# A streaming encoder step: 24 column units of the input projection as 12 pairs with seven quarter products, in a stage of their own ahead of the attention

## The chip, the cores and the metric

The kernel runs on one core of one Trainium2 chip. The core has a matrix engine (TensorE, PE in the profile, with its weight loads as PEld), a vector engine (VectorE, DVE), a scalar engine (ScalarE, ACT), a general one (GpSimd, POOL) and SyncE (SP), whose queue here issues most of the DMA transfers. Each engine works through its own instructions in order, and semaphores order the engines among each other. The metric is the device time of one execution in microseconds. Lower is better.

## What is computed

One layer of an encoder for 1024 prompt tokens and 64 sample tokens, all in float32. The tokens are normalised and multiplied by one input projection of 1024 x 6144. Its columns are the queries, keys, values and gate of two attention branches, then two channel gates.

```
def project(x, norm_w, w_in, q_norm_w, k_norm_w):
    h = rms_norm(x, norm_w) @ w_in
    sb_q, sb_k, sb_v, sb_z, cb_q, cb_k, cb_v, cb_z, g_sb, g_cb = jnp.split(h, SPLIT_POINTS, axis=-1)
    ...

def stick_breaking(q, k, v, q_pos, k_pos):
    z = jnp.einsum("bqhd,bkhd->bhqk", q, k).astype(jnp.float32) * ATTN_SCALE
    causal = k_pos[None, :] < q_pos[:, None]
    log_beta = jax.nn.log_sigmoid(z)
    log_keep = jnp.where(causal, jax.nn.log_sigmoid(-z), 0.0)
    suffix = lax.cumsum(log_keep, axis=3, reverse=True) - log_keep
    w = jnp.where(causal, jnp.exp(log_beta + suffix), 0.0)
    return jnp.einsum("bhqk,bkhd->bqhd", w.astype(v.dtype), v)

def merge(x, o_sb, z_sb, o_cb, z_cb, g_sb, g_cb, w_proj_sb, w_proj_cb, w_out):
    b_sb = (o_sb.reshape(lead + (WIDTH_SB,)) * jax.nn.silu(z_sb)) @ w_proj_sb
    b_cb = (o_cb.reshape(lead + (WIDTH_CB,)) * jax.nn.silu(z_cb)) @ w_proj_cb
    h = jax.nn.sigmoid(g_sb) * b_sb + jax.nn.sigmoid(g_cb) * b_cb
    return x + h @ w_out
```

The second branch ("cb") is a softmax over a band of at most 640 keys with a learned bias by distance. The keys and values of both branches are outputs too, in their natural layout (token by token).

## The kernel before

Every product keeps float32 accuracy by splitting each factor in a high and a low part, and by multiplying three times: high x high, high x low, low x high. The high part is an ACT copy, the low part a subtraction on DVE or POOL.

**Phase 1** (line 153 on) loads the tokens in nine tiles, normalises and transposes them into `xhl`, which stays on chip with the model dimension on the partitions (high and low, two halves of four blocks each, 1088 token columns). Beside that it computes eight groups of 256 columns (`NB`, line 160) in natural layout: the values of both branches, and the queries and keys of the second, which are normed per head, transposed and stored to DRAM (`d_qT`, `d_kT`).

**Units.** The other 32 blocks of 128 columns are "units" (`make_units`, line 120): k, q and the two gates z of each head pair, and the channel gates. A unit computes the transposed result: for each of three token ranges `CH` it runs 8 blocks x 3 matmuls, 24 of 384 or 320 columns, so 72 in all (line 563). Units are not a stage. They are a generator, `run_fill` (line 556), that gives one matmul at a time as a filler; after the last unit it continues with the first branch's output projection (`proj_units`, line 622, matmuls in line 661; 288 of them for each branch). A unit's weights are loaded two units ahead and split one unit ahead.

**Attention** (line 870 on) goes through 144 units of work: first branch ("sb", stick-breaking), then second ("cb", chunk band), each with four head pairs p, nine query tiles t (the sample tile first) and two heads. For unit i it emits in this order: `qk(i)` (scores, line 725 and 726; in sb the two sigmoids, lines 728 and 729; in cb the bias with a running minimum, line 731, and the exponential, line 735), half of the fillers, the product with the values of a finished tile pair (`av`, line 817), the transposes of unit i-2 (`tr`, line 777, copied to `wT` in turn by ACT and DVE, lines 786 and 788), `mid(i)` (in sb a scan and a multiply on DVE, lines 745 and 746; in cb a reciprocal and a scaling, lines 748 and 749), and the other fillers. The number of fillers follows the number of keys. In sb a filler's result goes straight to the place where it is used (`ev_k`, `ev_q`); `ev_k` also transposes k back for the natural-layout output, through the one buffer `ko` (line 519). In cb the tiles are loaded from DRAM by `load_q` and `load_k`. `until` makes sure that a head pair's own units are done before its attention begins.

**Phases 4 and 5** (line 910 on): the second branch's attention output is loaded, split (`make_og`, line 614, whose subtractions are line 620) and projected, with the rest of the fillers between; then the output projection with the residual (lines 990 to 992).

## Time and profile before

| what | value |
|---|---|
| runs of the kernel | 1035.84, 1037.40, 1037.94 us; median 1037.4 |
| profiled execution | span 1034.6 us from first to last instruction |
| granted TensorE clock | 0.999 of full speed on average |
| phase 1, from the start to the first filler | 230.2 us |
| weight splits on POOL, line 98 (tile `wlo`) | 51 operations, 127.6 us |
| matmuls of the units, line 563 | 2304 |

The profile is one execution. Its page lists each engine's busy time, the chain of work that ended last, and groups of equal instructions: line, engine, operation, out<-in, count | busy us, mean ns of one | idle time of the engine just ahead of them and who ended it. Busy times of matmuls overlap, as they are pipelined: the time that one costs is the distance from start to start, not its listed duration. A wait is put down to the one that came last. Idle time of an engine that does not set the end costs nothing.

### The profile page before, as it was taken

How to read it: one execution, taken by the hardware profiler on the slowest of the kernel's cores; microseconds unless marked ns; L12 is line 12 of the kernel's file. 1: busy time of each engine (PE TensorE's matmuls, PEld its weight loads, DVE VectorE, ACT ScalarE, POOL GpSimd, SP SyncE). 2: the span in 40 equal slices, each digit the busy share in tenths (PEclk: the TensorE clock that was granted, in tenths of full speed). 3: DMA queues.
4: the chain of work that ended last, by engine and by line, in shares of the span. 5: the costliest groups of instructions: out<-in, count | busy, mean ns of one | idle time of the engine just before them, and what ended most of it. 6: DMA issues, size and time to landing. Idle time of an engine off the chain costs nothing.

```text
span 1034.6 us, 19354 instructions
## 1 busy us (share of the span) xinstructions
PE 1014.8 (98%) x7412; PEld 968.4 (94%) x7412; DVE 543.9 (53%) x1069; ACT 418.7 (40%) x942; POOL 255.2 (25%) x277
## 2 busy tenths in 40 slices
PE   6999999999999999999999999999999999999998
PEld 5999999999999989999999999998988898999998
DVE  5416656402476556657655645565557685674111
ACT  5534443212454435444444454444445433552000
POOL 3227666202221111212121111101103211453110
PEclk9999999999999999999999999999999999999999
DMA  7654453745547323723384354665576834554322
GB/s 237 213 187 151 163 191 128 267 136 165 160 112 192 96 69 102 206 60 95 92 211 122 107 144 131 165 169 161 162 204 185 224 92 139 187 163 149 101 93 71
DMA packets 159660, 155.23 MB, mean 150 GB/s; under 512 B 23184, under 2 KB 144912, under 8 KB 159440
## 3 DMA queue, kind: packets, MB, share of 16 engines
q1 hardware_dynamic: 142800, 136.17, 44.2%
q10 hardware_dynamic: 16768, 17.83, 5.7%
q8 instruction: 58, 0.95, 0.4%
q14 instruction: 34, 0.28, 0.1%
HBM read 90.77 MB, written 49.81 MB: 136 GB/s over the span
## 4 chain that ended last, share of the span: by engine, by line
PE 91%; SPq 3%; DMA 2%; DVE 1%; ACT 1%; issue 1%; POOL 0%; ACTq 0%; DVEq 0%
PE acc L563 33%; PE acc L357 18%; PE acc L661 9%; PE o L817 7%; PE pt L777 6%; PE z L726 3%; PE z L725 3%; PE acc L992 3%; PE acc L991 3%; PE acc L990 3%; SPq L49 2%; DMA wrawx<-in_w_in_dram 1%; PE pk L301 1%; PE pt L229 1%; DMA d_ccbT<-hc 1%
## 5 line engine op out<-in xcount | busy, mean ns | idle before, releaser
L563 PE MATMUL acc<-xh,whi 128*128 128x384 f32 (+1 forms) x768 | 255.5, 333 | 0.1
L563 PE MATMUL acc<-xh,wlo 128*128 128x384 f32 (+1 forms) x768 | 255.3, 332 | 0.0
L563 PE MATMUL acc<-xl,whi 128*128 128x384 f32 (+1 forms) x768 | 254.8, 332 | 0.0
L98 POOL TENSOR_TENSOR wlo<-wraw,whi 128x1024 fp32r<-128x1024 f32 x51 | 127.6, 2501 | 440.2 <-ACT whi L91 386.1
L563 PEld LDWEIGHTS acc<-xh,wlo 128*128 128x128 f32 x768 | 144.8, 189 | 1.3
L563 PEld LDWEIGHTS acc<-xl,whi 128*128 128x128 f32 x768 | 144.5, 188 | 1.3
L563 PEld LDWEIGHTS acc<-xh,whi 128*128 128x128 f32 x768 | 144.5, 188 | 1.2 <-ACT sg L550 0.3
L745 DVE TENSOR_TENSOR_SCAN kp<-kp,imp 64x576 f32<-64x576 f32 (+8 forms) x72 | 110.6, 1536 | 5.1 <-ACT kp L728 5.1
L735 ACT ACTIVATE be<-be,sm 128x640 f32<-128x640 f32 (+5 forms) x72 | 50.8, 706 | 106.6 <-DVE sm L731 106.4
L728 ACT ACTIVATE kp<-z 128x384 f32<-128x384 f32 (+6 forms) x112 | 53.8, 480 | 97.3 <-PE z L726 87.6
L777 PE MATMUL pt<-ident,be 128*128 128x128 f32 (+2 forms) x608 | 88.8, 270 | 0.9 <-DVE wT L788 0.6
L786 ACT ACTIVATE wT<-pt 128x512 f32<-128x512 f32 (+3 forms) x104 | 52.9, 509 | 82.5 <-PE pt L777 81.6
L788 DVE COPY wT<-pt 128x256 f32<-128x256 f32 (+3 forms) x104 | 46.0, 442 | 70.3 <-PE pt L777 69.9
L777 PEld LDWEIGHTS pt<-ident,be 128*128 128x128 f32 (+2 forms) x608 | 68.7, 139 | 11.6 <-issue 7.1
L357 PE MATMUL acc<-whi,xh 128*128 128x256 f32 x256 | 75.2, 296 | 0.0
L357 PE MATMUL acc<-wlo,xh 128*128 128x256 f32 x256 | 71.7, 282 | 0.0
L357 PE MATMUL acc<-whi,xl 128*128 128x256 f32 x256 | 71.5, 281 | 0.0
L357 PE MATMUL acc<-whix,xh 128*128 128x256 f32 x256 | 70.9, 279 | 0.0
L357 PE MATMUL acc<-whix,xl 128*128 128x256 f32 x256 | 70.6, 278 | 0.0
L91 ACT ACTIVATE whi<-wraw 128x1024 fp32r<-128x1024 f32 x52 | 55.0, 1059 | 38.4 <-DVE y L996 35.8
L357 PE MATMUL acc<-wlox,xh 128*128 128x256 f32 x256 | 70.5, 277 | 0.0
L746 DVE TENSOR_TENSOR be<-be,kp 64x576 f32<-64x576 f32 (+8 forms) x72 | 62.3, 865 | 8.8
(157 smaller groups left out, 2168.7 us busy)
## 6 DMA issues: line engine op xcount, KB each, us to landing
wraw<-in_w_in_dram SPq DMA_DIRECT2D x40, 512.0 KB, 4.9
sq<-hl SPq DMA_DIRECT2D x32, 192.0 KB, 4.5
sq<-d_qT SPq DMA_DIRECT2D x32, 192.0 KB, 3.6
xt<-in_x_prompt_dram SPq DMA_DIRECT2D x8, 512.0 KB, 5.6
wrawx<-in_w_in_dram SPq DMA_DIRECT2D x8, 512.0 KB, 4.3
d_kT<-hl SPq DMA_DIRECT2D x8, 512.0 KB, 4.7
d_qT<-hl SPq DMA_DIRECT2D x8, 512.0 KB, 4.8
ks<-d_kT SPq DMA_DIRECT2D x16, 256.0 KB, 4.6
```

Of the source, the lines that this page charges most:

```text
L91: A.activation(h, raw, AF.Copy)
L98: (eng or G).tensor_tensor(out=l, in0=raw, in1=h[:].bitcast(F32), op=OP.subtract)
L357: TE.matmul(ps, x, w, start=m == 0, stop=m == len(steps) - 1)
L563: TE.matmul(ps[:, :b - a], w[:, k], xk(x, k)[:, a:b], start=k == 0 and n == 0, stop=k == KT - 1 and n == 2)
L661: TE.matmul(ps[:, :n], w[:, p, cw], g[:, a:e], start=p == 0 and m == 0, stop=p == NPAIR - 1 and m == 2)
L728: A.activation(kp[:r, x:y], z[:r, :m], AF.Sigmoid, scale=-0.125)
L735: A.activation(be[:r, :n], be[:r, :n], AF.Exp, bias=kp[:r, j:j + 1], scale=-1.0, accum_out=kp[:r, 2:3])
L745: V.tensor_tensor_scan(kp[:r, n - 1::-1], kp[:r, n - 1::-1], im[:, ::-1], 0.0, op0=OP.mult, op1=OP.add)
L746: V.tensor_tensor(out=be[:r, :n], in0=be[:r, :n], in1=kp[:r, 1:n + 1], op=OP.mult)
L777: TE.transpose(pt[:kr, x, :r], be[:r, kb * 128:kb * 128 + kr], ident[:r, :r])
L786: A.activation(w[:, sl:sl + m, q0:q0 + r], pt[:, :m, :r], AF.Copy)
L817: TE.matmul(o[hd * 64:hd * 64 + 64, c0:c1], vv[:kr, kb, hd * 64:hd * 64 + 64], wT[b, p, j, hd, s // 4][:kr, s % 4, c0:c1], start=si == 0, ...
```

## The change

The 12 k, q, z and first-gate pairs (two neighbouring units each, 256 columns) leave the fillers. Each pair is a product of a 256 x 1024 weight block and 1024 x 1088 tokens. It is cut in two along each side (columns 128 + 128, model dimension 512 + 512, tokens 544 + 544), and the four quarter results come from seven products of quarters instead of eight, after a scheme that adds and subtracts the factors first and the results afterwards. For this:

- the token columns of `xhl` are reordered (`xc`), so that each half holds 512 prompt and 32 sample tokens; `pieces` finds the token ranges again when results are stored;
- `make_t` forms four combinations of the token quarters on DVE, with their splits, beside the last groups of phase 1; phase 1's column groups and the step that prepares the bias rows change places for it, and the pool of phase 1 is closed early;
- `prep` forms the weight combinations on POOL and splits them (ACT, POOL), five products ahead; `load_raw` loads the raw halves;
- a new stage between phase 1 and the attention runs 12 x 7 products of 24 matmuls (12 with 256, 12 with 288 columns), in six PSUM banks; ACT and DVE combine the results, and `emit` stores them to DRAM, for k also in natural layout through `ko`. `up` is a pool of three buffers where no other number is given; `psF` has two buffers;
- the first branch's attention loads q and k from DRAM like the second, and `ev_k`, `ev_q`, `ev_silu`, `until` are gone. Eight units (the second channel gate) remain as fillers: one ahead of the attention, six in the first branch, one in the second with all 288 matmuls of the first output projection. The last unit is held back until the second branch has begun (`late["sb"]`). In the first branch ACT makes all copies to `wT`.

```diff
-        NB = [1024, 1280, 2560, 2816, 2048, 2304, 3072, 3328]
+        NB = [1024, 2560, 2816, 2048, 2304, 1280, 3072, 3328]
...
+        def make_t(tm, pool):
...
+            def sub(a, b, k):
+                d = pool.tile([128, HF], F32, name="d")
+                V.tensor_tensor(out=d, in0=x(0, *a[:1], k, a[1]), in1=x(0, *b[:1], k, b[1]), op=OP.subtract)
+                V.tensor_tensor(out=d, in0=d, in1=x(1, *a[:1], k, a[1]), op=OP.add)
+                V.tensor_tensor(out=d, in0=d, in1=x(1, *b[:1], k, b[1]), op=OP.subtract)
+                return d
...
+        def prep(n):
+
+            i, s = divmod(n, 7)
...
+            def total(x, y, op):
+                d = ws.tile([128, 4, 128], F32, name="ws")
+                G.tensor_tensor(out=d, in0=x, in1=y, op=op)
+                return d[:]
+
+            if s == 0:
+                src = r1[:, :, a]
+            elif s == 1:
+                sums[1] = total(r1[:, :, b], r2[:, :, b], OP.add)
+                sums[2] = src = total(sums[1], r1[:, :, a], OP.subtract)
...
+            A.activation(t[:, 0], src, AF.Copy)
+            G.tensor_tensor(out=t[:, 1], in0=src, in1=t[:, 0].bitcast(F32), op=OP.subtract)
+            blk[n] = t
+            if s == 4:
+                load_raw(2 * i + 3)
+            elif s == 6:
+                load_raw(2 * i + 4)
...
-                if (i, ti) == (4, 4):
+                if (i, ti) == (3, 8):
                     load_rb()
-                if i == 6 and ti > 0:
+                if i == 4 and ti > 0:
                     make_rb(ti - 1)
...
+        LEAD = 5
+        later = []
+
+        def soon(n, f):
+            later.append([n, f])
+
+        def step():
+            for e in later[:]:
+                e[0] -= 1
+                if e[0] < 0:
+                    later.remove(e)
+                    e[1]()
...
+        def emit(i, w, half, c, src, ps):
+
+            kind, _, arg = pairs[i]
+            n = XC[c][1] - XC[c][0]
...
+            h = up.tile([128, 2, 288], F32R, name="hl", bufs=2)
+            A.activation(h[:, 0, :n], src[:, :n], AF.Copy)
+            V.tensor_tensor(out=h[:, 1, :n], in0=src[:, :n], in1=h[:, 0, :n].bitcast(F32), op=OP.subtract)
+            p = arg + w
+            dst = (d_kT if kind == "k" else d_qT)["sb"][p]
+            soon(0, lambda: stores(rdma, half, c, h[:, :, :n], dst[:]))
+            if kind == "q":
+                return
...
+            def out():
+                pt = psF.tile([128, 512], F32, name="acc")
+                ko = up.tile([128, 3, 128], F32, name="ko", bufs=1)
+                cols = slice(p * 128, (p + 1) * 128)
+                for t in range(2):
+                    TE.transpose(pt[:, t * 128:(t + 1) * 128], kf[:, t * 128:(t + 1) * 128], ident)
+                if c == 1:
+                    TE.transpose(pt[:32, 256:384], kf[:, 256:288], ident)
+                    A.activation(ko[:32, 2], pt[:32, 256:384], AF.Copy)
+                    SP.dma_start(o_sbk_s[32 * half:32 * half + 32, cols], ko[:32, 2])
+                A.activation(ko[:, :2], pt[:, :256].rearrange("p (t c) -> p t c", c=128), AF.Copy)
+                a = half * 512 + c * 256
+                SP.dma_start(o_sbk_p[a:a + 256, cols].rearrange("(t q) c -> q t c", q=128), ko[:, :2])
+            soon(1, out)
...
+        BANK = "1231223"
+        for i in range(len(pairs)):
+            bank, s1, u2, u3 = {}, {}, {}, {}
+            for s in range(7):
+                n = 7 * i + s
+                prep(n + LEAD)
...
+                step()
+                w = blk.pop(n)
+                for c, (a, b) in enumerate(XC):
+                    m = b - a
+                    if s < 3:
+                        bank[BANK[s], c] = psB.tile([128, 512], F32, name=f"b{BANK[s]}{c}")
+                    ps = bank[BANK[s], c]
+                    for k in range(4):
+                        for e, (hl_, x) in enumerate(((0, 0), (0, 1), (1, 0))):
+                            TE.matmul(ps[:, :m], w[:, hl_, k], right[s](x)[:, k, a:b], start=s < 3 and k == 0 and e == 0,
+                                      stop=k == 3 and e == 2, skip_group_check=s > 2)
+                    if s == 0:
+                        s1[c] = up.tile([128, 288], F32, name="s1")
+                        A.activation(s1[c][:, :m], ps[:, :m], AF.Copy)
+                    elif s in (1, 4):
+                        u = up.tile([128, 288], F32, name="u2" if s == 1 else "u3")
+                        (u2 if s == 1 else u3)[c] = u
+                        V.tensor_tensor(out=u[:, :m], in0=ps[:, :m], in1=s1[c][:, :m], op=OP.add)
+                    elif s == 3:
+                        emit(i, 0, 0, c, ps, True)
...
     def fill(n):
+        n += owed[0]
+        owed[0] = 0
         while n > 0:
+            if prog[0] == len(units) - 2 and "sb" not in late:
+                owed[0] = n
+                return
...
-                if flip[0] % 2:
+                if flip[0] % 2 or b == "sb":
                     A.activation(w[:, sl:sl + m, q0:q0 + r], pt[:, :m, :r], AF.Copy)
...
-    until(1)
-    fill(48)
-    FP = 170
-    n_sb = 72 * FILL_SB - 48
-    n_cb = 72 * (len(units) - 2 - FILL_SB) + FP
+    fill(72)
+    FP = 288
+    n_sb = 72 * 6
+    n_cb = 72 + FP
```

## The prediction

> **What bounds the kernel now.** I read the page's busy table first, then the busy time by stage, then the chain of waits, then the groups of single engines. The page, top lines:

> ```profile
> span 1034.6 us, 19354 instructions
> ...
> PE 1014.8 (98%) x7412; PEld 968.4 (94%) x7412; DVE 543.9 (53%) x1069; ACT 418.7 (40%) x942; POOL 255.2 (25%) x277
> ```

> TensorE (PE) is busy through 98% of the span, VectorE (DVE) through half. That is an average; the same table by stage (phase 1; stick-breaking attention up to its last DVE multiply; chunk-band attention up to the last value product; closing stages), columns stage, length, then busy time and count of PE, PEld, DVE, ACT, POOL, the granted clock, DMA share, GB/s:

> ```profile
> 0.00:230.20 230.20, 218.64 (x1840) 216.89 (x1841) 102.60 (x214) 90.67 (x213) 101.76 (x117) 1.00 0.56 187
> 230.20:634.95 404.75, 404.25 (x2700) 381.91 (x2699) 229.15 (x274) 179.01 (x397) 68.59 (x97) 1.00 0.45 125
> 634.95:869.80 234.85, 232.75 (x1686) 211.05 (x1684) 147.06 (x467) 106.51 (x254) 38.00 (x34) 1.00 0.61 171
> 869.80:1034.60 164.80, 159.16 (x1192) 158.52 (x1191) 65.13 (x115) 42.51 (x78) 46.80 (x29) 1.00 0.41 130
> ```

> Both attention stages keep PE full, because the projection matmuls (line 563) and the first output projection (line 661) are poured as filler between the attention's own steps. How many of each lie there (same table for line 563, the two attention stages, then for line 661, the second):

> ```profile
> 230.20:634.95 404.75, 320.93 (x1754) 288.68 (x1755) 1.00 0.45 125
> 634.95:869.80 234.85, 112.40 (x552) 89.54 (x550) 1.00 0.61 171
> ```
> ```profile
> 634.95:869.80 234.85, 44.37 (x218) 35.58 (x218) 1.00 0.61 171
> ```

> Busy times overlap, so the pace of a matmul is read from unbroken runs in the chain of waits (start, length, count):

> ```profile
> 194.91 35.50 PE acc L357 x304
> ...
> 314.96 2.20 PE acc L563 x15
> ...
> 441.91 3.30 PE acc L563 x19
> ```

> 256 columns take 35.50/304 = 116.8 ns, 320 take 2.20/15 = 146.7, 384 take 3.30/19 = 173.7. A filler of line 563 or 661 (two of three have 384 columns) takes 164.7 ns on average.

> **The change, part by part.**

> *Products.* 24 units of 72 matmuls go: each 48 x 173.7 + 24 x 146.7 ns = 11.86 us, together 284.6. 12 pairs of 7 products come; a product is 12 matmuls of 256 and 12 of 288 columns; 288 is not in the trace, between 256 and 320 lies 131.7. A product takes 2.98 us, a pair 20.9, all 250.5. TensorE alone gains 34.1: 1034.6 - 34.1 = 1000.5 if no new wait comes. The 36 k transposes only move.

> *Phase 1.* The token differences (56 DVE operations of 128x544, 16 ACT copies) lie beside the last two and a half column groups; the bias rows move from the seventh group into the fifth, where DVE already norms. DVE has room (102.60 of 230.20). Cost between 0 and 6 us if its lag reaches a PSUM tile; I take 0.

> *Weight blocks.* Prices of the side engines:

> ```profile
> L98 POOL TENSOR_TENSOR wlo<-wraw,whi 128x1024 fp32r<-128x1024 f32 x51 | 127.6, 2501 | 440.2 <-ACT whi L91 386.1
> ...
> L745 DVE TENSOR_TENSOR_SCAN kp<-kp,imp 64x576 f32<-64x576 f32 (+8 forms) x72 | 110.6, 1536 | 5.1 <-ACT kp L728 5.1
> L735 ACT ACTIVATE be<-be,sm 128x640 f32<-128x640 f32 (+5 forms) x72 | 50.8, 706 | 106.6 <-DVE sm L731 106.4
> ...
> L788 DVE COPY wT<-pt 128x256 f32<-128x256 f32 (+3 forms) x104 | 46.0, 442 | 70.3 <-PE pt L777 69.9
> ...
> L91 ACT ACTIVATE whi<-wraw 128x1024 fp32r<-128x1024 f32 x52 | 55.0, 1059 | 38.4 <-DVE y L996 35.8
> ...
> L746 DVE TENSOR_TENSOR be<-be,kp 64x576 f32<-64x576 f32 (+8 forms) x72 | 62.3, 865 | 8.8
> ```

> A pair needs 11 POOL operations of 512 elements, half of 2501 ns each: 13.8 us, plus about three waits of 0.7 for ACT: 16 of 20.9. Five products of lead cover it; without them each late block would cost up to 2.6. I take 0 here, and 2 us for the stage's start, where the first new tiles wait for phase 1's last stores.

> *The two k pairs.* This is where I expect the largest loss. Each k pair writes eight transposed outputs. One takes a PSUM buffer of the pair of "acc" buffers, an ACT copy into `ko`, of which there is one, and a store; the next ACT copy waits until that store has landed. And the results' own tile `hl` has two buffers, also held until their stores land. The tile `ko` in the trace, and the stores of `hl` to DRAM:

> ```profile
> L527 ACT ACTIVATE ko<-pt x12: 392/492/525, 239.1 to 518.6; 128x384 f32<-128x384 f32 x8, 128x256 f32<-128x256 f32 x4
> L528 SPq DMA_DIRECT2D out_dram<-ko x12: 383/394/629, 240.4 to 522.7; - x12
> L525 ACT ACTIVATE ko<-pt x4: 278/278/280, 272.9 to 518.5; 64x128 f32<-64x128 f32 x4
> ...
> DMA to landing us min/median/max: 1.8/2.9/5.1
> ```
> ```profile
> d_kT<-hl SPq DMA_DIRECT2D x8, 512.0 KB, 4.7
> ```

> Per product from the fourth on, two outputs and two results: block copy 0.53, first output copy 0.39, its store 2.9, second output's copies 0.67, then on SP, in order, its two issues and the first store of `hl`, 0.4 each (1.2), that store's landing (half the 512 KB of the row; between 1.8 and 4.7, I take 3.0), two result copies 0.8: 9.5 us, against 2.98 of matmuls. ACT works in order, so this is one chain. TensorE is held by the two "acc" buffers: the transposes of step n wait for the copies of step n-1. Three steps are held: the first by about 3.5, since the chain starts beside the product before, two by 9.5 - 2.98 = 6.5, less 0.6 each for the transposes themselves. That is about 15 a pair, 30 for both. Behind the waiting ACT copy stand the next block copy and the results' copies, and DVE's additions behind those; behind the stores on SP stand the next weight loads. Both have five products of lead, so nothing more is late. Ends: with the shortest landing of 1.8 for both stores the cycle is 7.2 and the pair loses 10; with 5.1 and 4.7 it is 13.4 and 23. A gain is excluded, since a wait is only added. The q pairs have `hl` alone; their lag ends before a bank is needed again: 0.

> *Stick-breaking attention.* PE there, without filler: 404.75 - 1754 x 0.1647 = 115.9. The new filler is 72 ahead and 432 inside: 83.0. PE sum 198.9. DVE's sum is 110.6 + 62.3 = 172.9 by the scan and multiply rows, and the value products a little more. ACT takes over DVE's half of the copies of line 788 (about half of 46.0) and loses the block copies of 16 units (17 us) and their evacuations: near its 179.01 of now. So PE stays the longest on the whole, but query tiles 0 to 2 have little PE work and are set by DVE; with the pipeline's first fill I add 5 (0 to 15). The k and q tiles now come from DRAM; the first unit needs 12 transfers, 12 x 0.4 + 4.7 = 9.5 us, and the 72 fillers (11.9 us) cover them; without that cover they cost the 9.5.

> *Chunk-band attention.* Its filler falls from 552 + 218 to 360. PE without filler: 234.85 - 770 x 0.1647 = 108.0; with 360: 167.3. But here a unit is a serial chain on DVE: bias and minimum (731), exponential on ACT (735), reciprocal (748), scaling (749), and the next unit's 731 stands behind 749 in DVE's order. The groups of DVE, then the one left of ACT:

> ```profile
> L749 DVE TENSOR_SCALAR be<-be,sm 128x640 f32<-128x640 f32 (+5 forms) x72 | 40.9, 568 | 2.5
> L731 DVE CUSTOM_DVE_ANT_0 be<-z,bias 128x320 f32<-128x320 f32 (+5 forms) x72 | 34.7, 482 | 13.6 <-PE z L726 10.0 <-DMA bias<-d_rb 3.1
> L731 DVE CUSTOM_DVE_ANT_0 be<-z,bias,sm 128x320 f32<-128x320 f32 (+1 forms) x40 | 21.7, 543 | 6.1 <-DVE sm L731 0.5
> ...
> L748 DVE RECIPROCAL sm<-sm 128x1 f32<-128x1 f32 (+1 forms) x72 | 11.4, 159 | 16.0 <-ACT be L735 15.2
> ...
> L731 DVE DVE_READ_ACCUMULATOR2_ANT sm<- 128x1 f32 (+1 forms) x112 | 9.1, 81 | 0.0
> ```
> ```profile
> L735 ACT ACTIVATION_READ_ACCUMULATOR be<-be,sm 128x1 f32 (+1 forms) x72 | 13.4, 186 | 0.0
> ```

> Chain: 40.9 + 34.7 + 21.7 + 11.4 + 9.1 + 50.8 + 13.4 = 182.0, 2.53 a unit, over PE's 167.3 (2.32 a unit). DVE is busy 147.06 in this stage now, 117.8 of it in this chain; the other 29.3 can run while DVE waits for ACT (50.8 + 13.4). Some will not: I take 8 of them, between 0 and 29. At the start the bias tile is late, as now, and the filler that hid it is gone, since the last unit waits for the stick-breaking stage's stores:

> ```profile
> 638.02 0.45 DVE L731 CUSTOM_DVE_ANT_0 be<-z,bias 64x288 f32<-64x288 f32 x1 [3.07 <-DMA bias<-d_rb]
> ```

> 3.1 at the start, 4.3 from the last 749 to the end. Against that, some 4.4 of PE's last stick-breaking work runs beside the start. 182 + 8 + 3.1 + 4.3 - 4.4 = 193.0, that is 25.7 more than PE's sum; ends 18 and 47 by the 0 and 29.

> *Closing stages.* 118 fillers that were left for here are gone (406 - 288): -19.4. They covered the gating of the last attention outputs. DVE's splits for the three token ranges:

> ```profile
> 876.60 1.94 DVE L620 TENSOR_TENSOR og<-ot,og 128x384 fp32r<-128x384 f32 x2
> ...
> 884.55 0.87 DVE L620 TENSOR_TENSOR og<-ot,og 128x384 fp32r<-128x384 f32 x1 [2.23 <-ACT og L619]
> ...
> 888.06 2.15 DVE L620 TENSOR_TENSOR og<-ot,og 128x320 fp32r<-128x320 f32 x2 [2.24 <-ACT og L619]
> ```

> The first range is ready at 878.5, 8.7 after the last value product; its 24 matmuls take 4.2, then 2.7 until 885.4, then 0.6: 12.0 idle (8 to 13). 164.8 - 19.4 + 12.0 = 157.4.

> **Sum.** 230.2 + (250.5 + 2 + 30) + (198.9 + 5) + 193.0 + 157.4 = 1067.0. The profiled execution had 1034.6; the median of the runs is 1037.4, 2.8 more for what lies around the span. 1069.8, so 1070.

> [...] TensorE now hardly ever idles. Where it did, at the start, matmuls of 256 columns came slower:

> ```profile
> 14.60 1.05 PE L357 MATMUL acc<-wlo,xs 128*128 128x256 f32 x4
> 15.45 1.01 PE L357 MATMUL acc<-wlox,xs 128*128 128x256 f32 x4
> ```

> Four in 0.85 us, 212 ns each against 116.8, though the profile's clock column reads 1.00. [...]

> **Rivals.**

> (A) *The k outputs drain beside the matmuls.* For it: sixteen such copies hide now, with the same single `ko`. Against: they are spread over 280 us now, eight stand in 12 us then. 1070 - 30 = 1040.

> (B) *TensorE stays the bound: the side chains are no longer than the matmuls beside them.* Place: chunk-band attention and the k pairs. It decides where DVE's 2.53 us a unit falls under 2.32, which overlap of its steps could do, and where the output chain runs ahead of the transposes. For it: PE fills 232.75 of 234.85 now. Against: only since there were 770 fillers. Price: both terms go, 1070 - 30 - 25.7 = 1014; faster. The gap of 12 stays.

> (C) *Idle time slows the matmuls after it.* After idling, 212 - 116.8 = 95 ns are lost per matmul over about 5 us, some 2.3 us each time. Four holds of the k pairs, the start of the chunk-band stage and the closing gap: 6 x 2.3 = 14, 1084.

> **How the numbers follow.** Forecast 50%, A 17%, B 18%, C 15%. The likeliest alone: 1048 to 1092 (its largest terms reach 20 lower or 16 higher for the k pairs, 8 lower or 21 higher for the chunk-band stage, and will hardly all fall to one side). The range must take in A and most of B: 1020 to 1092. This kernel's measurement can tell about 0.2% (2 us) from no change. Faster: B, and the lower edge of A, 22%; same 5%, from A; slower 73%.

> **What would show it.** The new stage longer than 270 us, with ACT's `ko` copies waiting for their own stores and PE idle at the transposes of the k pairs (under 260: A). The chunk-band stage near 195 us with PE under 90% busy and ACT's exponentials back to back with DVE's (168: B). PE idle about 8 us after the last value product. The stick-breaking stage about 204 us, PE over 90%. Slow matmuls right behind each hold would show C. A new stage near 250 and a chunk-band stage under 180 would make the forecast wrong.

## Result and the profile after

The changed kernel takes 1197.39 us (median of 4 runs, 1195.04 to 1201.87) against 1036.62 for the kernel before beside it: 1.1555 times as long, 95% interval 1.153 to 1.1581. The forecast was 1070, the range 1020 to 1092. Slower was right; the size was not. The page of the profiled execution, top lines:

```profile
span 1196.0 us, 20767 instructions
...
PE 1064.5 (89%) x7704; PEld 996.7 (83%) x7704; DVE 589.4 (49%) x1201; ACT 480.3 (40%) x1126; POOL 363.8 (30%) x389
```

TensorE was to be relieved of work, and is busy 50 us longer than before (1064.5 against 1014.8) at a lower share. Busy time by stage (phase 1, new stage, stick-breaking, chunk-band, closing; columns as before, the granted clock behind the five engines):

```profile
0.00:266.35 266.35, 235.40 (x1841) 230.93 (x1841) 143.76 (x270) 99.83 (x230) 103.29 (x123) 0.95 0.48 161
266.35:572.03 305.68, 276.19 (x2059) 271.44 (x2058) 80.57 (x187) 97.84 (x226) 166.84 (x130) 0.93 0.36 108
572.03:809.73 237.70, 211.27 (x1422) 188.64 (x1421) 161.66 (x165) 147.93 (x366) 25.92 (x80) 0.92 0.57 146
809.73:1031.35 221.62, 190.14 (x1266) 156.15 (x1266) 143.97 (x470) 92.06 (x228) 21.28 (x27) 0.93 0.55 148
1031.35:1196.00 164.65, 151.51 (x1121) 149.51 (x1120) 59.48 (x109) 42.65 (x78) 46.49 (x29) 0.98 0.41 129
```

| stage | predicted | measured | over |
|---|---|---|---|
| phase 1 | 230.2 | 266.4 | 36.2 |
| new stage | 282.5 | 305.7 | 23.2 |
| stick-breaking | 203.9 | 237.7 | 33.8 |
| chunk-band | 193.0 | 221.6 | 28.6 |
| closing | 157.4 | 164.7 | 7.3 |
| sum | 1067.0 | 1196.0 | 129.0 |

Every stage is over by 7 us or more, and every clock is under 1.00, where all four rows of before show 1.00. Phase 1 shows what that means: its some 1840 matmuls are the same, but PE is busy 235.40 instead of 218.64 us, 16.8 more. The other 19.4 of the 36.2 are idle time. Against the sums that the prediction made from paces at full clock, PE's busy time in the next three stages is over by 276.2 - 250.5 = 25.7 (some 5 of it the 40 k transposes), 211.3 - 198.9 = 12.4 and 190.1 - 167.3 = 22.8. With phase 1 that makes some 70 us of slower matmuls. The granted clock allows for that much: its mean of 0.940 over 1196.0 us is 72 us short of full speed.

### The profile page after: what moved, and what is told of

Read it like the earlier page. It is cut to its first block, busy times and chain, and to the rows that moved or that the text cites. A ratio compares the mean times of both kernels' runs of the same rounds, so it can differ in the third digit from the quotient of the medians.

```text
span 1196.0 us, 20767 instructions
## 1 busy us (share of the span) xinstructions
PE 1064.5 (89%) x7704; PEld 996.7 (83%) x7704; DVE 589.4 (49%) x1201; ACT 480.3 (40%) x1126; POOL 363.8 (30%) x389
## 4 chain that ended last, share of the span: by engine, by line
PE 46%; issue 13%; DMA 13%; DVE 11%; POOL 7%; ACT 7%; SPq 3%; ACTq 0%; DVEq 0%; POOLq 0%
PE acc L435 9%; PE b L592 9%; PE o L973 5%; PE acc L716 5%; PE pt L933 4%; POOL ws L378 3%; PE acc L1149 3%; PE acc L1148 2%; PE acc L1147 2%; DVE be L887 2%; SPq L51 2%; ACT be L891 2%; DMA out_dram<-ko 2%; PE z L881 2%; PE z L882 2%
## 5 line engine op out<-in xcount | busy, mean ns | idle before, releaser
L114 POOL TENSOR_TENSOR wlo<-wraw,whi 128x1024 fp32r<-128x1024 f32 x27 | 66.7, 2470 | 199.6 <-ACT whi L107 191.9
L901 DVE TENSOR_TENSOR_SCAN kp<-kp,imp 64x576 f32<-64x576 f32 (+8 forms) x72 | 99.9, 1387 | 15.0 <-ACT kp L884 14.8
L942 ACT ACTIVATE wT<-pt 128x512 f32<-128x512 f32 (+3 forms) x156 | 72.7, 495 | 46.2 <-PE pt L933 45.9
L973 PE MATMUL o<-wT,vp 128*64 128x256 f32 (+1 forms) x608 | 77.3, 369 | 11.1 <-DVE wT L944 5.6
L973 PEld LDWEIGHTS o<-wT,vp 128*64 128x64 f32 x608 | 48.7, 141 | 38.5 <-ACT wT L942 10.0
L881 PE MATMUL z<-ks,sq 128*128 128x320 f32 (+4 forms) x192 | 66.2, 347 | 8.4 <-DMA sq<-d_qsbT 4.5
L716 PE MATMUL acc<-xh,whi 128*128 128x384 f32 (+1 forms) x192 | 70.0, 364 | 0.0
L600 DVE TENSOR_TENSOR u<-b,s 128x256 f32<-128x256 f32 (+1 forms) x48 | 20.2, 437 | 100.0 <-PE b L592 60.1
L716 PE MATMUL acc<-xh,wlo 128*128 128x384 f32 (+1 forms) x192 | 68.7, 358 | 0.0
L716 PE MATMUL acc<-xl,whi 128*128 128x384 f32 (+1 forms) x192 | 68.3, 356 | 0.0
L882 PE MATMUL z<-ks,sq 128*128 128x320 f32 (+4 forms) x192 | 65.6, 344 | 0.0
## 6 DMA issues: line engine op xcount, KB each, us to landing
wraw<-in_w_in_dram SPq DMA_DIRECT2D x41, 512.0 KB, 4.2
xt<-in_x_prompt_dram SPq DMA_DIRECT2D x8, 512.0 KB, 5.2
wrawx<-in_w_in_dram SPq DMA_DIRECT2D x8, 512.0 KB, 4.3
d_kcbT<-hl SPq DMA_DIRECT2D x8, 512.0 KB, 4.8
d_qcbT<-hl SPq DMA_DIRECT2D x8, 512.0 KB, 6.1
```

The costliest lines, as they stand in the source:

```text
L114: (eng or G).tensor_tensor(out=l, in0=raw, in1=h[:].bitcast(F32), op=OP.subtract)
L716: TE.matmul(ps[:, :b - a], w[:, k], xk(x, k)[:, a:b], start=k == 0 and n == 0, stop=k == KT - 1 and n == 2)
L881: TE.matmul(z[:r, :m], s[:, 2 * hd, q0:q0 + r], ks[:, hd, o + x:o + y], start=True, stop=False)
L882: TE.matmul(z[:r, :m], s[:, 2 * hd + 1, q0:q0 + r], ks[:, hd, o + x:o + y], start=False, stop=True)
L901: V.tensor_tensor_scan(kp[:r, n - 1::-1], kp[:r, n - 1::-1], im[:, ::-1], 0.0, op0=OP.mult, op1=OP.add)
L942: A.activation(w[:, sl:sl + m, q0:q0 + r], pt[:, :m, :r], AF.Copy)
```

## The experiments

The first four follow the stages in order, then come the clock by itself, and versions with several edits.

**Phase 1.** Waits of PE, then of ACT, from 150 us to the end of phase 1 (in all, times, longest), of the changed kernel:

```profile
PE acc L435 <- ACT vst L253: 12.1, 7, 2.6
...
ACT t0h L331 <- DVE d L338: 17.0, 4, 9.1
ACT t2h L331 <- DVE d L338: 13.2, 4, 3.8
```

ACT stands in the copies of the token differences until DVE's chain has made them, and the value eviction that frees PE's PSUM tile is behind it. The first edit issues these copies, and the subtractions that need them, one token tile later:

```diff
-                put(0, k, d)
+                lo(jobs)
+                jobs = [(0, k, d)]
                 yield
+                hi(jobs)
```

> The changed kernel with one edit in phase 1: of the token differences, the ACT copy of a high part and the DVE subtraction of its low part are issued one token tile later than the DVE chain that makes the difference, so that ACT, which works in order, no longer stands in that copy while a value tile waits for its eviction. Same operations, same count. My theory (ACT waits for DVE in these copies, and the value evictions behind them hold PE): phase 1 goes from 266 us to 236 (232 to 242), the 2 us holes of PE between 185 and 242 us go, granted clock of the stage 0.99 instead of 0.95, the whole 1197 to about 1167. Rival 1 (the added work of ACT and DVE as such, or the bias rows and the new order of column groups): phase 1 stays above 260. Rival 2 (the holes go but the slow matmuls do not depend on them): phase 1 near 249.

Measured: 1176.04 us (ratio 1.1343, 1.1323 to 1.1363); phase 1 250.0, clock 0.98. 16.4 of the 36.2 us went; the theory had about 30. What stood behind one of the holes left is in the timeline of this run, first DVE, then PE:

```profile
200.11 0.72 DVE L336 TENSOR_TENSOR t0l<-d,t0h 128x544 fp32r<-128x544 f32 x1
200.75 0.41 DVE L241 TENSOR_TENSOR fl<-acc,fl 64x256 f32<-64x256 f32 x1
```
```profile
201.21 0.38 PE L451 MATMUL acc<-whi,xh 128*128 128x256 f32 x1 [2.39 <-DVE fl L241]
```

The fold of the sample tile (241) waits in DVE's order behind the difference chain, and PE for the fold. So the second edit, on top of the first, spreads the 56 DVE operations over the tiles:

```diff
+            for m, _ in enumerate(one()):
+                if m % 3 == 2:
+                    yield
+                    flush_high()
```

> As e1_t_copies_later, and the 56 DVE operations of the token differences are issued three to a token tile of the last two and a half column groups instead of four to seven at a time to every second one. Same operations and count. e1 took phase 1 from 266 to 250 and left five holes of PE of 1.2 to 2.4 us, the longest where the sample tile's fold stood behind five DVE operations of 0.72 us. Theory (all of phase 1's loss is this order of DVE and ACT, and the half-paced matmuls behind the holes): phase 1 is 231 to 240, clock 0.99, the whole 1156 to 1168. Rival (what is left in e1 comes from the bias rows or the weight splits, which this does not touch): phase 1 stays at 246 to 252.

Measured: 1165.9 us (1.1245, 1.1216 to 1.1274). Phase 1 of this run:

```profile
0.00:238.55 238.55, 223.51 (x1840) 220.84 (x1841) 143.50 (x270) 99.76 (x230) 104.44 (x123) 1.00 0.54 180
```

DVE and ACT do as much as in the changed kernel (143.50 and 99.76 us), in another order, and 27.8 of the 36.2 us are gone with the clock back at 1.00. The stretch with the differences shows how, in the changed kernel and then in this run:

```profile
185.00:242.00 57.00, 40.01 (x253) 37.67 (x251) 44.50 (x56) 17.00 (x32) 7.07 (x3) 0.81 0.19 58
```
```profile
180.00:238.55 58.55, 57.18 (x477) 56.78 (x476) 45.28 (x58) 21.64 (x43) 11.97 (x6) 1.00 0.35 109
```

DVE is as busy in both, 78 and 77%. The changed kernel issues the differences four or six to a token tile, in twelve tiles, which are some 34 us of matmuls at full pace, so PE is held to DVE's pace: 253 matmuls, where 477 lie beside the same work when it is spread. Most of the loss was this crowding and not the amount of work, and the rivals fall. The other 8.4 us of phase 1 stay open.

**The k and q pairs.** Busy time by pair in the changed kernel, each from the first matmul of the pair, the first five and then the other seven:

```profile
266.35:301.17 34.82, 25.58 (x185) 24.26 (x184) 6.47 (x17) 10.45 (x26) 20.17 (x16) 0.92 0.37 113
301.17:329.51 28.34, 25.95 (x176) 25.47 (x174) 5.92 (x15) 8.21 (x21) 12.06 (x10) 0.85 0.41 122
329.51:365.79 36.28, 26.86 (x186) 25.28 (x184) 9.78 (x24) 10.16 (x25) 15.77 (x13) 0.84 0.39 118
365.79:394.55 28.76, 26.22 (x176) 25.56 (x174) 5.95 (x15) 8.21 (x21) 12.09 (x10) 0.85 0.40 120
394.55:422.41 27.86, 23.30 (x170) 23.07 (x169) 10.07 (x23) 10.37 (x21) 16.02 (x13) 0.88 0.37 108
422.41:572.03 149.62, 148.28 (x1179) 147.81 (x1178) 42.38 (x96) 50.44 (x112) 90.73 (x71) 1.00 0.33 100
```

The last row is seven gate pairs at full clock, 21.4 us each. The first five are k, q, k, q and the gate pair behind them, 156.1 us where five times 20.9 are 104.5. The k pairs lose 13.9 and 15.4 us, the q pairs 7.4 and 7.9, the gate pair 7.0. All but about 1 us of a q pair's loss lies in its first two products, where the last outputs of the k pair ahead of it are transposed. (The expectations below set the bounds elsewhere, inside the last product of a k pair, so that their figures put the end of a k pair into the q pair.) Waits of ACT there, then of PE:

```profile
ACT wlo L401 <- POOL ws L378: 30.8, 9, 4.7
ACT ko L562 <- DMA out_dram<-ko: 23.5, 8, 4.9
ACT hl L542 <- DMA d_ksbT<-hl: 19.9, 7, 3.6
ACT hl L542 <- DMA d_qsbT<-hl: 13.2, 6, 3.3
```
```profile
PE acc L559 <- ACT ko L564: 11.4, 6, 3.8
PE acc L559 <- DVE u L607: 5.7, 2, 3.5
PE acc L559 <- DVE kf L552: 5.5, 3, 3.0
PE b L592 <- DVE u L600: 5.5, 3, 4.6
```

PE waits 28.1 us, 22.6 of them at the transposes (line 559); the rest of the 51.6 is slower matmuls and the transposes themselves. ACT's longest wait is another one, for POOL's weight sums. But in the seven gate pairs it is longer still, 42.9 us in 13 waits, and PE waits only 1.3 us there, so this wait alone does not hold PE. Three `ko` together with four `hl` need 29.25 KB a partition where 25.34 are left, so each tile gets more buffers by itself.

Two edits, each alone:

```diff
-                ko = up.tile([128, 3, 128], F32, name="ko", bufs=1)
+                ko = up.tile([128, 3, 128], F32, name="ko", bufs=3)
```
```diff
-            h = up.tile([128, 2, 288], F32R, name="hl", bufs=2)
+            h = up.tile([128, 2, 288], F32R, name="hl", bufs=3)
```

> The changed kernel with three buffers instead of one for the transposed k output tile ko; the result tile hl keeps its two. As the prediction had it, ACT stands in the second copy into ko until the first one's store has landed (23.5 us in 8 waits there now). Theory 1 (ko is the larger part of the k pairs' cost): the four first pairs, 27.2, 34.6, 28.1 and 36.1 us, become about 23, 27, 23 and 28, the new stage 305 becomes 280 to 288, the whole about 1177. Theory 2 (hl holds ACT just as long once ko is free, since its stores are queued behind on SP): the stage is 297 to 306, the whole above 1188.

> The changed kernel with three buffers instead of two for the result tile hl of the k and q pairs; ko keeps its one. ACT waits 33 us in 13 waits for hl's stores now, in the q pairs too, which I had costed at nothing. Theory 1 (ko is the larger part): the stage stays at 298 to 306. Theory 2 (hl is): the first five pairs lose some 20 together, the stage is 280 to 290, the q pairs' bank waits (PE for DVE's addition, 4.6 us at one place) go. Neither: both buffers have to go together, and each alone gives under 5.

Measured: 1176.6 us with three `ko` (1.1358, 1.1317 to 1.1398), new stage 289.9, the first pairs 30.4, 24.8, 29.5, 27.9 and 27.5; 1183.03 with three `hl` (1.1417, 1.1379 to 1.1456), new stage 293.8, pairs 33.3, 27.0, 32.0, 29.3 and 21.9. Neither theory has it alone: `ko` is worth 15.8 us, `hl` 11.9, and half of `hl`'s gain lies in the gate pair behind the last q pair. With both, in the version with nine pairs below, the five still take 131.3 us, so some 27 of the 51.6 stay.

**The stick-breaking stage.** DVE's longest wait, and the SP queue just before it ended, in the changed kernel:

```profile
DVE zt L976 <- DMA zt<-d_zsb: 23.2, 4, 10.8
```
```profile
603.84 2.98 SPq L51 DMA_DIRECT2D sq<-d_qsbT  x4
606.87 0.59 SPq L951 DMA_DIRECT2D zt<-d_zsb  x1
```

The first gate tile is issued behind every transfer of k and q, and DVE, in order, stands in the gating multiply with the next scan behind it. The first try moved eight transfers to ACT's queue:

```diff
+    Q[0] = A
     load_k("sb", 0, 0)
     load_q("sb", 0, 0)
+    Q[0] = SP
```

> The changed kernel with the first unit's placing of k and q for the prompt (load_k and load_q of pair 0, 8 transfers) issued from ACT's queue instead of SP's, at the start of the stick-breaking stage. My theory (SP issues some 50 transfers in a row, 0.6 us each, from 578 to 609 us, and the first gate tile zt stands last among them, so DVE waits 10.8 us for it and PE 6.8): SP is done about 5 us earlier, the first pair's 67 us becomes 59 to 63 and the stage 238 becomes 229 to 234, the whole 1189 to 1193. Rival (DVE's scans set the first pair, the queue is covered): stage within 2 us of 238. Third (ACT's issues delay the sigmoids): stage longer.

Measured: 1191.23 us (1.1478, 1.1453 to 1.1504), the stage 235.8. That decides nothing: PE got a new hole, where a filler's eviction stood on ACT behind the new transfers:

```profile
PE acc L718 <- ACT sg L704: 11.7, 1, 11.7
```

The second try leaves the queue as it is and asks for the gate tiles earlier:

```diff
+    load_z(*zq.pop(0))
     load_k("sb", 0, 1)
     load_q("sb", 0, 3)
...
-                load_z(*avq[-1])
+                if zq:
+                    load_z(*zq.pop(0))
```

> The changed kernel with the gate tiles zt of the attention loaded one value product earlier (three buffers instead of two), the first of them ahead of the first k and q tiles on SP's queue. In the changed kernel DVE waits 23.2 us in 4 waits for such loads in the stick-breaking stage and 6.2 us in 3 in the chunk-band stage, and works in order, so the scans behind them are late. e3, which moved eight transfers to ACT's queue instead, only moved the wait: PE's hole of 6.8 us at the start became one of 11.7 behind an ACT eviction queued after those transfers. Theory (SP's queue at the stage's start, by the gate tile that stands last in it): the waits of zt for DMA go, the stick-breaking stage becomes 220 to 230 us instead of 238, the chunk-band stage 216 to 219 instead of 222, the whole 1177 to 1187. Rival (the first q and k tiles themselves are as late as zt, so PE waits for them instead): stage 234 to 240, whole above 1191.

Measured: 1163.78 us (1.1213, 1.1192 to 1.1233), more than expected. Stick-breaking and chunk-band stage of this run, and what is left of the wait in the first:

```profile
570.32:781.64 211.32, 202.05 (x1422) 180.58 (x1421) 162.69 (x165) 146.96 (x365) 26.08 (x80) 0.97 0.64 165
781.64:996.58 214.94, 186.45 (x1266) 151.93 (x1266) 143.83 (x470) 92.00 (x228) 21.15 (x27) 0.95 0.57 152
```
```profile
DVE zt L976 <- DMA zt<-d_zsb: 1.8, 1, 1.8
```

26.4 of the 33.8 us go with the late gate tiles, 9 of them by PE's shorter busy time (211.27 to 202.05) at a higher clock (0.97 instead of 0.92). The run moves all gate tiles and gives them a third buffer; what the first one does by itself, 10.8 of the 23.2 us of waits, it does not separate. Of the 7.4 that remain, PE's two waits for the first q tiles, 4.0 and 2.5 us, are the largest idle part.

**The chunk-band stage.** Is it short of filler? Three sigmoid pairs go back as filler:

```diff
-    for j in range(0, KT, 2):
+    for j in range(0, 2, 2):
         pairs.append(("sig", 4096 + 128 * j, d_g["sb"][j:j + 2]))
...
-    n_cb = 72 + FP
+    n_cb = 72 * 7 + FP
```

> Three of the four sigmoid pairs are taken out of the new stage and their six column units go back as single units into the filler of the chunk-band stage (432 fillers more there, 71 us of TensorE at 164.7 ns). All else as in the changed kernel. My theory (the chunk-band stage is set by the chain DVE - ACT - DVE of its units, which TensorE now waits for; filler lies beside it for nothing until TensorE's sum of 108 + 792 x 0.1647 = 238 passes the chain): the new stage loses 3 x 20.9 = 63 us, the chunk-band stage grows from 222 to 238 to 248, granted clock there 0.99 or more, the whole 1197 to about 1155. Rival (TensorE's own work sets that stage too, the slow matmuls come from elsewhere): the stage grows by 71 to 293 and the whole is 8 us longer, 1205.

Measured: 1153.33 us (1.113, 1.11 to 1.1159); the stage:

```profile
740.67:986.22 245.55, 238.66 (x1697) 215.76 (x1695) 146.06 (x470) 105.79 (x252) 35.42 (x33) 0.99 0.57 160
```

71 us of matmuls more make it 24 us longer. Of the other 47, 24.6 lie in time that PE had been idle (31.5 us before, 6.9 now), and 22.5 come back because the matmuls are faster, with the clock at 0.99: PE's busy time grows by 48.5 only. With only 360 fillers TensorE does not bound the stage. Whether it is the serial chain of a unit, as the prediction had it, two further edits ask. The first issues a unit's scaling behind the next unit's bias step; the second also puts the gating multiply at the end of the iteration:

```diff
-        if i < len(seq):
-            mid(i)
+        if 0 < i <= len(seq) and seq[i - 1][0] == "cb":
+            mid(i - 1)
+        if i < len(seq) and seq[i][0] == "sb":
+            mid(i)
```
```diff
+        while gates:
+            gates.pop(0)()
         fill(m - m // 2)
```

> The changed kernel with one edit in the chunk-band stage: the reciprocal and the scaling of a unit are issued on DVE after the bias-and-minimum of the next unit instead of before it, so that ACT's exponential lies beside DVE's next step. Same operations and count. My theory (the stage is set by the serial chain DVE - ACT - DVE of its units, 217 of its 222 us; DVE's own busy time is 144, TensorE's sum by nominal paces 167): the stage falls to 180 to 200 us, the whole to 1157 to 1177. Rival 1 (TensorE's order, the value products' waits, sets the stage): 215 to 222, whole above 1190. Rival 2 (it falls to TensorE's sum at once): 167 to 175, whole about 1147.

> As e9_cb_scale_later, and the gating multiply of a finished value product is issued on DVE after the scaling of the unit before instead of ahead of the wT copies, in both attention stages. Same operations and count. Theory (in the chunk-band stage the loop between the two in-order engines sets the time: DVE stands in the gating multiply for TensorE's value products, TensorE stands in the transposes for DVE's scaling): DVE's waits of 25 us for the value products shrink under 10, the stage falls from e9's 211 to 185 to 198, the stick-breaking stage from 238 to 225 to 236 as its zt loads no longer hold the scan, the whole to 1155 to 1177. Rival (the halved matmul pace sets it): chunk-band stage 206 to 212, whole above 1180.

Measured: 1187.59 us (1.1443, 1.1409 to 1.1478), stage 210.8, and 1173.37 (1.1325, 1.1283 to 1.1367), stage 212.4. DVE's waits in the stage of the first, then of the second:

```profile
DVE zt L976 <- PE o L973: 22.4, 15, 4.8
...
DVE wT L944 <- PE pt L933: 6.4, 13, 1.5
```
```profile
DVE wT L944 <- PE pt L933: 19.4, 15, 2.5
DVE zt L978 <- PE o L973: 11.2, 6, 4.2
```

Loosening the chain of a unit in this way gives 11 us, not the 20 to 40 expected. With it loosened DVE waits for PE's value products, and with that moved, for PE's transposes: the wait changes its place, 28.8 us in two rows and 30.6. PE's clock stays at 0.93 and 0.94. The theory of e11 falls for this stage. Its time for the whole comes all the same, by another stage: the stick-breaking stage falls to 221.5, further than expected. That a loop between two in-order engines with slow matmuls in it is what is left is argued, not shown.

**The clock by itself.** The kernel before, with dummy copies on ACT ahead of one eviction a column group, so that PE runs out of PSUM tiles:

```diff
+                if ti == 5:
+                    for _ in range((0, 17, 19, 21, 23, 17, 19, 21)[i]):
+                        A.activation(dum, dum, AF.Copy)
                 got = evac_nat(i, t, ps)
```

> The kernel before, with dummy ACT copies of a 128x512 tile (about 0.5 us each) ahead of one eviction in each column group from the second to the eighth of phase 1 (17, 19, 21, 23, 17, 19, 21 of them), so that TensorE runs out of PSUM buffers and stands still for some 0.5 to 4 us, once per group, in a kernel that has none of the changed one's other work. Theory (a hole of about 2 us is enough to bring matmuls of 256 columns from 117 ns to about 210 ns for the next 3 to 7 us): behind the holes of 2 us and more the rows show 210 ns, behind those under 1 us 117 ns; the whole is longer than 1037 by the holes and about as much again. [...] Rival 2 (the fall of the granted clock belongs to the new stage's work): all matmuls stay at 117 ns and the loss is the sum of the holes.

Measured: 1104.33 us (1.0655, 1.0627 to 1.0683). The holes came out at 3.2 to 11.8 us, too long to show whether 2 us are enough; behind all seven, 13 to 26 matmuls came 210 to 220 ns apart. So a second run with 15, 7, 8, 9, 10, 14 and 16 copies:

> As e5_before_with_holes, whose holes came out at 3.2 to 11.8 us, all seven with 16 to 26 matmuls of 256 columns at 210 to 220 ns behind them, while one hole of 1.96 us in its closing stage had none. Now 15, 7, 8, 9, 10, 14 and 16 dummy copies, for holes of some 1 to 3.5 us. Theory (about 2 us is enough in some cases, depending on how much idle time falls near it, as in the changed kernel): holes of 2 us and more show 210 ns for 3 to 5 us in most cases, those under 1.5 us in none. [...]

Measured: 1067.58 us, one run, 30.7 more than the kernel before beside it (1036.84). Its line 359 in the 5 us behind a hole of 1.89 us (stretch, length, PE busy and count, PEld, clock):

```profile
70.65:75.65 5.00, 4.80 (x25) 4.62 (x26) 0.66 0.39 114
```

The kernel before has this in the same place:

```profile
70.65:75.65 5.00, 4.81 (x41) 4.63 (x40) 1.00 0.95 308
```

25 matmuls where 41 go. Behind four of the run's eight holes the pace was halved (1.89, 3.13, 3.25 and 4.53 us), behind the other four it was not (1.27, 1.48, 1.76 and 2.60). So a hole of 1.89 us can be enough, and the length alone does not decide. What goes with it is shown by the clock: in the traces of before and of the changed kernel all its 51 changes lie at marks 3.41 us apart. From mark to mark in this run, around the hole of 1.89 us and then the one of 2.60 (all engines):

```profile
67.37:70.78 3.41, 1.52 (x14) 1.32 (x13) 0.00 (x0) 3.28 (x8) 0.00 (x0) 1.00 0.00 0
70.78:74.19 3.41, 3.41 (x17) 3.41 (x18) 0.69 (x1) 1.80 (x4) 2.29 (x1) 0.50 0.48 155
74.19:77.60 3.41, 3.41 (x31) 3.41 (x31) 0.00 (x0) 0.39 (x1) 0.09 (x1) 1.00 0.65 160
162.93:166.34 3.41, 1.80 (x16) 1.60 (x14) 0.62 (x2) 3.31 (x9) 0.11 (x1) 1.00 0.00 0
166.34:169.75 3.41, 2.43 (x21) 2.43 (x22) 2.86 (x9) 2.06 (x5) 3.16 (x5) 1.00 0.00 0
```

The shorter hole lies in one step and leaves PE idle through 1.89 of its 3.41 us, 55%; the longer one lies across a mark and leaves 1.61 and 0.98. In the traces of before and of the changed kernel a step at half clock followed each of the 21 recorded full-clock steps with more than 58% idle, five of the eight between 45 and 58%, and none of the 572 with less. In this run the holes cost their own length, and half of the time that the half pace lasts behind them: the holes are 19.9 us together and the half-paced time 21.4, which makes 30.6 of the 30.7 us. The theory holds, with three of the four holes over 2 us and none under 1.5. Rival 2 of the first of the two runs falls: it happens in the kernel before, without the new stage's products.

**Together.** Nine pairs, the spread differences, three `ko` and three `hl`, the earlier gate tiles, six units back as filler, and 170 instead of 288 fillers of the first output projection:

```diff
-    n_sb = 72 * 6
-    n_cb = 72 + FP
+    n_sb = 72 * 7
+    n_cb = 72 * 6 + FP
```

> All that helped together: e6's spread token differences; three buffers each for ko and hl (u2 and u3 give up one each); the gate tiles earlier; nine pairs instead of twelve, their six units back as filler, one of them in the stick-breaking stage and five in the chunk-band stage; 170 instead of 288 of the first output projection's matmuls in the chunk-band stage, the other 118 left for the closing stage, as in the kernel before. If the parts add up as measured alone: phase 1 239, new stage 244 - 28 = 216, stick-breaking 230 to 238 (12 us of filler more, zt's waits gone), chunk-band 222 to 230, closing 165: 1075 to 1090, still slower than 1037. Rival (the holes slow what is behind them, so parts taken away together give more than their sum): under 1070. To beat the kernel before, the new stage would have to take 190 and the stick-breaking stage 205.

Measured: 1069.25 us (1.0323, 1.0302 to 1.0344). Its stages took 239.3, 218.1, 218.4, 221.2 and 170.6. That is just the rival's time, but hardly by its reason. Only the stick-breaking stage came out well below its range of 230 to 238, and that was set before e7's result: e7's 211.3 and 12 us of filler make 223. The kernel before stays ahead. On top of that e9's edit, and other queues in the new stage:

```diff
-            SP.dma_start(raws[n], w_in[h * 512:(h + 1) * 512, c:c + 256].rearrange("(k p) n -> p k n", p=128))
+            G.dma_start(raws[n], w_in[h * 512:(h + 1) * 512, c:c + 256].rearrange("(k p) n -> p k n", p=128))
...
-                SP.dma_start(o_sbk_p[a:a + 256, cols].rearrange("(t q) c -> q t c", q=128), ko[:, :2])
+                A.dma_start(o_sbk_p[a:a + 256, cols].rearrange("(t q) c -> q t c", q=128), ko[:, :2])
```

> e8 with e9's edit, and in the new stage the raw weight loads issued from POOL's queue, the ko stores from ACT's queue, and four buffers for hl (kf has one, sg two): in e8's k and q pairs SP stood up to 3.3 us waiting to issue a weight load for POOL's sums, with hl's stores behind it, and ACT waited 24 us in 6 waits for those stores. Theory: the five first pairs, 26.4, 25.1, 25.8, 25.5 and 26.9 us, become 21 to 23 (new stage 218 to about 200), the chunk-band stage 221 becomes 208 to 215 (TensorE's sum by nominal paces is 207), the whole 1069 becomes 1038 to 1050. Rival (POOL's or ACT's issues are as late as SP's, and TensorE already fills the chunk-band stage): 1060 to 1075.

Measured: 1065.69 us (1.0281, 1.026 to 1.0301); new stage 212.6, its first pairs 31.0, 22.7, 26.0, 23.0 and 22.8, chunk-band stage 219.0. That is the rival's range. Last come the pairs without what was moved with them: six gate pairs, k and q back in the fillers and placed from SBUF:

```diff
-    for p in (0, 2):
-        pairs += [("k", 512 + 128 * p, p), ("q", 128 * p, p)]
...
+    for p in range(NPAIR):
+        units += [("ev_k", 512 + 128 * p, (p,)), ("ev_q", 128 * p, (p,))]
```

> Only six pairs are left in the stage of their own, the four silu pairs and two of the sigmoid pairs; k and q, four sigmoid units and the eight plain units are filler of the attention stages again (20 units), k and q placed from SBUF as in the kernel before, in column chunks of 384, 160, 256 and 288; with e6's spread token differences, zt earlier, and e11's order on DVE. By nominal paces six pairs save 6 x 2.84 = 17 us of TensorE's 1034.6; phase 1 is 8 longer (e6), the new stage's start costs about 6. Theory (the loss belongs to what was moved with the pairs: with gate pairs alone and filler enough, TensorE is the bound again): each pair 20.5 to 22 but the first, both attention stages with PE over 97% busy, the whole 1025 to 1045, about that of the kernel before, 1037. Rival (the pairs as such cost more than they save, by block sums and side engines): above 1060.

Measured: 1089.74 us (1.0509, 1.0485 to 1.0534). The first pair, the five others, and the two attention stages:

```profile
238.06:266.16 28.10, 24.14 (x171) 23.91 (x170) 6.82 (x16) 10.66 (x22) 20.45 (x16) 0.88 0.35 106
266.16:373.99 107.83, 106.09 (x843) 105.62 (x842) 34.36 (x76) 35.63 (x78) 62.76 (x48) 1.00 0.32 95
```
```profile
373.99:689.28 315.29, 286.55 (x2085) 263.08 (x2084) 187.32 (x213) 170.78 (x421) 39.94 (x86) 0.96 0.47 124
689.28:920.46 231.18, 223.97 (x1615) 202.67 (x1613) 143.28 (x462) 104.17 (x252) 32.62 (x32) 0.99 0.59 164
```

Five pairs do what they should, 107.8 us, 21.6 each, against 23.7 for two units. But with the first one the six take 135.9, and phase 1 is 7.9 longer: 143.8, where twelve units take 142.3. So by themselves the pairs gain nothing here. The greater loss lies elsewhere: the attention and closing stages are 51.6 us longer than in the kernel before without these twelve units. The stick-breaking stage has 28.7 us of idle PE at clock 0.96, half of them waiting for the sample q tiles, which in this column order come in more and smaller transfers (that this is the reason is not shown):

```profile
PE z L982 <- DMA sqs<-hl: 14.4, 2, 7.8
```

So the rival's time came, for the smaller part by its reason. No version that was run beats the kernel before.

## Why the prediction was right or wrong, point by point

- **Products: right.** The last seven gate pairs take 21.1 to 22.2 us in the changed kernel where 20.9 was worked out.
- **Phase 1, "I take 0" (0 to 6): wrong, 36.2.** This is the step that failed worst. It read DVE's 102.60 of 230.20 busy as room, an average over the phase, and took the differences to lie beside two and a half column groups. They were issued in twelve token tiles, where DVE needed 58 us (from 184.4 to 242.7) beside some 34 us of matmuls, with ACT copies waiting for it, ahead of evictions on both in-order engines. e6 takes 27.8 of the 36.2 away with the same busy times.
- **The k pairs, 15 each: right mechanism, mis-sized.** PE waited at the transposes, ACT for `ko`'s and `hl`'s own stores. But the outputs held on into the q pairs: 29.3 us were lost in the k pairs and 13.5 in the first two products behind them, 42.8 where 30 were taken, with slow matmuls behind each hold, which had been taken at nothing. The q pairs' `hl`, costed at 0, holds the gate pair behind them, by 6 us of its 7.0 (e2b). The start was taken at 2.
- **Weight blocks at 0: held** in the seven gate pairs, where PE waits 1.3 us in all; for the k and q pairs it is not shown apart from the other waits.
- **Stick-breaking, 198.9 + 5: wrong by 33.8.** The sentence that 72 fillers cover the first unit's 12 transfers left out the others that stand on SP's queue ahead of the first gate tile. e7 shows it: 211.3 with the gate tiles asked for earlier.
- **Chunk-band, 193: right that filler's loss uncovers it, mis-sized and partly mis-named.** e4 shows that TensorE no longer bounds it. The serial chain was to be nearly all of the 25.7 us over TensorE's sum; the one way of loosening it that was run gives 11 (e9), and zt's loads asked for earlier give 6.7 (e7). PE's busy time is 22.8 over its sum, by slower matmuls, which the prediction took at nothing here. What sets the stage's 221.6 as a whole stays open.
- **Closing, 157.4: 164.7.** The hole behind the last value product came (5.7 us at first, where 8.7 were worked out), and slow matmuls with it, a clock of 0.98.
- **Rivals.** A and B fell: the k outputs don't hide, and TensorE isn't the bound. C named the mechanism that runs through all stages, and its price of 2.3 us a hole was about right (1.8 to 3.1 us behind the holes of e5b). Its count of six holes was not: it took holes where the prediction had put waits, and the waits it had costed at nothing each brought theirs. The trace of the changed kernel has 25 stretches at half clock, and some 70 us of slower matmuls came where C had 14.

The kind of step that failed is the same in phase 1, for the q pairs' stores and for the gate tiles: a side engine or a queue was costed by its total, where the order of its instructions set what PE waited for. That slower came out right rests on the terms for the k pairs and the chunk-band stage, which were right in kind. More than half of the 129 us over, 36.2 and 33.8, lies in the two stages whose added cost was taken at 0 and at 5.

## What to carry to other kernels

A side engine that is busy half the time is no cover (DVE with 102.60 of 230.20 us in phase 1, where 36.2 were lost): take its share over the stretch where the new work is issued, and list, for each new operation, what is queued behind it on its in-order engine or DMA queue, and who waits for that. Price a hole of 2 us or more in TensorE at its length and some 2 to 3 us again, since the matmuls behind it can run at half pace (in e5b that cost half of 21.4 us behind four of eight holes, 2.7 each). Before taking work out of a stage that it fills, work out what the stage is without it: 71 us of matmuls put back into the chunk-band stage made it only 24 us longer.

## What the hardware showed that was not expected

In phase 1 of the changed kernel the second operation of a difference chain took 2.8 us instead of 0.72 three times out of eight, each time with a weight split on POOL beside it. DVE, then POOL:

```profile
194.57 2.80 DVE L337 TENSOR_TENSOR d<-d,xl 128x544 f32<-128x544 f32 x1
197.41 0.72 DVE L338 TENSOR_TENSOR d<-d,xl 128x544 f32<-128x544 f32 x1
```
```profile
194.44 2.35 POOL L114 TENSOR_TENSOR wlox<-wrawx,whix 128x1024 fp32r<-128x1024 f32 x1 [16.63 <-ACT whix L107]
```

DVE began 0.13 us after POOL and ended 0.58 after it. The other two cases are alike: 2.83 us beside a split of 2.37 and 2.80 beside one of 2.34, each begun 0.13 us after POOL and ended 0.59 after it. The five with no POOL operation beside them took 0.72 to 0.73 us. Why it is so is not shown.
